# Scores inside blocks of four tokens from one set of products in a hybrid recurrence and attention block

## The chip, the cores and the metric

The kernel runs on one core of one Trainium2 chip. The metric is device microseconds of one execution. A core has TensorE (PE; PEld is its weight load), VectorE (DVE), ScalarE (ACT), GpSimd (POOL) and a queue engine (SP) that issues the transfers. Each engine takes its instructions strictly in order.

## What is computed

A sequence of 1024 tokens (model width 1024) goes through an RMSNorm, one large projection, a gated linear recurrence of 8 heads, a sliding-window attention of 16 heads, a gated merge, an output projection and a last RMSNorm. The change lies in the recurrence. Cut to it, the reference is

```python
f = lb + (1.0 - lb) * jax.nn.sigmoid(hf)      # forget factor, per token and key channel
k_h = 1.0 - f
q_h = jax.nn.silu(hq)
...
b = jnp.cumsum(g_, axis=2)                    # g_ = log f
diff = b[:, :, :, None, :] - b[:, :, None, :, :]
decay = jnp.exp(jnp.where(causal[:, :, None], diff, -jnp.inf))
scores = jnp.einsum('bhtd,bhsd,bhtsd->bhts', q_, k_, decay)
o_intra = jnp.einsum('bhts,bhsv->bhtv', scores, v_)
```

The score of query t and earlier key s is a sum over 128 channels of q times k times the product of all forget factors behind s up to t.

## The kernel before

All products of a weight matrix with the activations are done in float16 with a high and a low part: three passes of eight 128x128 weight tiles (`mm_T`, `mm_tok`; line L302 and L314), 512 or 256 columns each. One unit of 256 weight columns follows the other: for each pair of heads the units `pf` (forget factors), `pq` (queries) and `pv` (values), then gates (`pg`), the attention's keys (`pk`) and values, and so on. ACT and DVE turn each unit's float32 weights into the two float16 parts (`wh` at L235, `wl` at L236) after DVE has found their largest value (`wmx`, L204) and POOL has reduced it over partitions (`p_r`, L121). The product banks are three (`pj`), so a unit's fourth product needs the first one read out.

The recurrence of one head is the generator `hgrn(h)`. It works in the background: `Background.step` lets some of it be issued behind each pass of the foreground. Then the framework's scheduler sets each engine's final order, so every change in the amount of work on an engine can move the others' places.

Inside a head the sequence is eight blocks of 128 tokens (the second half of the token axis lies in reverse order, which is why positions appear in two halves of 512). Scores inside a block are made by distances: `diagonal` multiplies k and q of the same token (L550), and `level` does one set of products for each c of 1, 2, 4, ..., 64 (L582): queries in the second half of each group of 2c tokens with keys in the first half. Between the levels q and k are multiplied in place by products of forget factors (L590 once, then L570 and L573 for each level; the products `hp` come from L540), so that each holds its decay up to the group's border. Before each level ACT copies the half of k and of q that it needs side by side into `kq` (L567, L568, one buffer of three). DVE then keeps what is wanted of each product by a mask, into the score tile `sc` (L554 for the diagonal with mask `idm`, L587 for a level with `lmask[c]`). POOL makes the masks in `setup_masks` at the start. All matrix products of the recurrence are float32 128x128; each is two MATMUL and two LDWEIGHTS records in the trace, and a level is four of them, so eight MATMUL records.

After the seven levels come transposes of k (`tp`, L607), state updates (`up`, L619), a chain of seven state steps on DVE (L627), the readout (`op`, L637 and L639) and its norm (`ms`, `rb`).

Of the kernel before, what the change touches and what calls it, by code (L numbers as in the profile page):

```python
# [14 lines left out]
F32 = mybir.dt.float32  # L15
F16 = mybir.dt.float16
I32 = mybir.dt.int32
U8 = mybir.dt.uint8
AF = mybir.ActivationFunctionType
ALU = mybir.AluOpType  # L20
# [3 lines left out]
P = 128  # L24
# [4 lines left out]
HALF = 512  # L29
# [6 lines left out]
NH = 8  # L36
DH = 64
ZS = 2.0**-19
ARATE = 0.5
ARATE2 = 0.8  # L40
CUT = 4
# [18 lines left out]
def view(ap, off, dims):  # L60

    base = ap[:, off : off + 1]
    return bass.AP(tensor=base.tensor, offset=base.offset, ap=[base.ap[0]] + dims)
# [3 lines left out]
def hybrid_block(ctx: ExitStack, tc: _tile.TileContext, x, norm_w, w_in, hlb, hnw, wbh, sinks, wba, w_out, fnw, out):  # L67
    nc = tc.nc
    V, A, G, PE, SP = nc.vector, nc.scalar, nc.gpsimd, nc.tensor, nc.sync

    const = ctx.enter_context(tc.tile_pool(name="const", bufs=1))
    wp = ctx.enter_context(tc.tile_pool(name="wp", bufs=3))
    sl = ctx.enter_context(tc.tile_pool(name="sl", bufs=24))
    tiny = ctx.enter_context(tc.tile_pool(name="tiny", bufs=4))
# [5 lines left out]
    def nm(s):  # L80
        uid[0] += 1
        return f"{s}{uid[0]}"

    def slot(name, shape=None, dt=F32):
        return sl.tile(shape or [P, 1024], dt, tag="s4", name=nm(name))

    def small(name, w, dt=F32, bufs=4):
        return tiny.tile([P, w], dt, tag=f"{name}_{w}", name=nm(name), bufs=bufs)

    def bank(name, pool=None):  # L90
        pool = pool or sm
        return pool.tile([P, HALF], F32, tag="bk", name=nm(name))
# [42 lines left out]
    ident = const.tile([P, P], F32, name="ident")  # L135
# [226 lines left out]
    lbc = const.tile([P, NH], F32, name="lbc")  # L362
# [1 line left out]
    snk = const.tile([P, 16], F32, name="snk")  # L364
    amask = const.tile([P, 2, 256], F32, name="amask")
    lmask = {}
    idm = const.tile([P, P], U8, name="idm")
    imask = idm[:].rearrange("p (o t) -> p o t", o=1).broadcast_to([P, 4, P])
    sc_bufs = []

    def setup_bounds(dif):

        A.activation(dif[:], dif[:], AF.Sigmoid)
        V.tensor_copy(oml[:], dif[:])
        V.tensor_scalar(lbc[:], dif[:], -1.0, 1.0, ALU.mult, ALU.add)

    def setup_masks():
        for c in (1, 2, 4, 8, 16, 32, 64):
            f = small("mk", P, bufs=1)
            G.memset(f[:], 1.0)  # L380
            J = 64 // c
            fv = f[:].rearrange("p (j e i) -> p j e i", j=J, e=2)
            G.affine_select(fv, fv, [[-2 * c, J], [-c, 2], [0, c]], ALU.is_ge, 0.0, base=0, channel_multiplier=1)
            G.affine_select(fv, fv, [[2 * c, J], [c, 2], [0, c]], ALU.is_ge, 0.0, base=c - 1, channel_multiplier=-1)
            mk = const.tile([P, HALF], U8, name=f"lmask{c}")
            G.tensor_copy(
                mk[:].rearrange("p (m t) -> p m t", m=4),
                f[:].rearrange("p (o t) -> p o t", o=1).broadcast_to([P, 4, P]),
            )
            lmask[c] = mk  # L390
        G.tensor_copy(idm[:], ident[:])
        G.memset(amask[:], 0.0)
        m0, m1 = amask[:, 0], amask[:, 1]

        G.affine_select(m0[:, 0:P], m0[:, 0:P], [[-1, P]], ALU.is_ge, NEG, base=0, channel_multiplier=1)
        G.affine_select(m0[:, P:256], m0[:, P:256], [[-1, P]], ALU.is_ge, NEG, base=P - 2, channel_multiplier=-1)

        G.affine_select(m1[:, 0:P], m1[:, 0:P], [[1, P]], ALU.is_ge, NEG, base=-P, channel_multiplier=1)
        G.affine_select(m1[:, P:256], m1[:, P:256], [[1, P]], ALU.is_ge, NEG, base=0, channel_multiplier=-1)
        for i in range(3):  # L400
            s = slot("sc")
            G.memset(s[:], 0.0)
            sc_bufs.append(s)
# [122 lines left out]
    def hgrn(h):  # L526

        hd = heads[h]  # L530
        q, k, f, v = hd["q"], hd["k"], hd["f"], hd["v"]
        sc = sc_bufs.pop(0)

        hp = tiny.tile([P, 1024], F32, tag="hp", name=nm("hp"), bufs=2)
# [8 lines left out]
            src, at = hp, do  # L543
        prod = hp[:, at : at + NB]

        def diagonal(b):
            lv = bank("lv")
            for j in range(4):
                cs = slice((4 * b + j) * P, (4 * b + j + 1) * P)
                PE.matmul(lv[:, j * P : (j + 1) * P], k[:, cs], q[:, cs], start=True, stop=True)  # L550
            return lv

        def keep_diagonal(b, lv):
            V.copy_predicated(  # L554
                sc[:, b * HALF : (b + 1) * HALF].rearrange("p (c t) -> p c t", c=4), imask,
                lv[:].rearrange("p (c t) -> p c t", c=4),
            )

        def dims_of(c):
            n = 256 // c  # L560
            return [[HALF + c, 2], [2 * c, n], [1, c]], [[HALF - c, 2], [2 * c, n], [1, c]], [[c, 2], [2 * c, n], [1, c]]

        def side_by_side(c):

            kdims, qdims, mdims = dims_of(c)
            kq = tiny.tile([P, 2, HALF], F32, tag="kq", name=nm("kq"), bufs=3)
            A.activation(view(kq[:, 0], 0, mdims), view(k, 0, kdims), AF.Copy)  # L567
            A.activation(view(kq[:, 1], 0, mdims), view(q, c, qdims), AF.Copy)  # L568
            (src, po), n, nb = areas[c.bit_length() - 1], 256 // c, HALF // c
            V.tensor_tensor(  # L570
                view(k, 0, kdims), view(k, 0, kdims), view(src, po + 1, [[nb - 1, 2], [2, n], [0, c]]), ALU.mult
            )
            V.tensor_tensor(  # L573
                view(q, c, qdims), view(q, c, qdims), view(src, po, [[nb + 1, 2], [2, n], [0, c]]), ALU.mult
            )
            return kq

        def level(kq):
            lv = bank("lv")
            for m in range(4):  # L580
                ms = slice(m * P, (m + 1) * P)
                PE.matmul(lv[:, ms], kq[:, 0, ms], kq[:, 1, ms], start=True, stop=True)  # L582
            return lv

        def keep_level(c, lv):
            _, qdims, mdims = dims_of(c)
            V.copy_predicated(view(sc, c, qdims), view(lmask[c], 0, mdims), view(lv, 0, mdims))  # L587

        lv0, lv1 = diagonal(0), diagonal(1)
        V.tensor_tensor(q[:], q[:], f[:], ALU.mult)  # L590
        kq = side_by_side(1)
        yield 1800, 6500
        keep_diagonal(0, lv0)
        keep_diagonal(1, lv1)
        for c in (1, 2, 4, 8, 16, 32, 64):
            lv = level(kq)
            if c < 64:
                kq = side_by_side(2 * c)
            yield 900, LAT
            keep_level(c, lv)  # L600

        kT = slot("kT", [P, NB, P])
        for b in range(2):
            tp = bank("tp")
            w = 4 - b
# [24 lines left out]
        o, osq = kT[:].rearrange("p c d -> p (c d)"), k  # L630
        for b in range(2):
            ps = bank("op")
            for j in range(4):
                p = 4 * b + j
# [19 lines left out]
        for b in range(2):  # L654
            rb = bank("rb")
            for j in range(4):
                p = 4 * b + j
# [16 lines left out]
    def u_ak(blk):  # L674
        c = blk.outscale()
        ainv["k"] = const.tile([P, 1], F32, name="akc")
        V.tensor_scalar(ainv["k"][:], c[:], 0.125 / ZS / ZS, None, ALU.mult)
        for g in range(4):
            kk[g] = slot("kk", [P, 2, T], F16)
        for half in range(2):  # L680
            sli = slice(half * HALF, (half + 1) * HALF)
            for j in range(2):
                ps = bank("pk", pj)
                mm_T(ps[:], blk, j, xact, half * HALF)
                for e in range(2):
                    g = 2 * j + e
                    rows = slice(e * DH, (e + 1) * DH)
                    for d in range(2):
                        A.activation(kk[g][d * DH : (d + 1) * DH, 0, sli], ps[rows], AF.Copy, scale=ZS)
                    for d in range(2):  # L690
                        V.scalar_tensor_tensor(
                            kk[g][d * DH : (d + 1) * DH, 1, sli], ps[rows], ZS, kk[g][rows, 0, sli], ALU.mult,
                            ALU.subtract,
# [4 lines left out]
    def u_av(blk):  # L698
        c = blk.outscale()
        ainv["v"] = const.tile([P, 1], F32, name="avc")  # L700
        V.tensor_scalar(ainv["v"][:], c[:], 1.0 / ZS, None, ALU.mult)
        for e in range(2):
            va[e] = slot("va", [P, NB, 256], F16)
        for tp in range(NB // 2):
            ps = bank("pv", pj)
            psv = ps[:].rearrange("p (t n) -> p t n", t=2)
            for i in range(2):
                mm_tok(psv[:, i], blk, xact, (2 * tp + i) * P)
                bg.step(2780)
            A.activation(va[0][:, 2 * tp : 2 * tp + 2, :], psv, AF.Copy, scale=ZS)  # L710
            V.scalar_tensor_tensor(
                va[1][:, 2 * tp : 2 * tp + 2, :], psv, ZS, va[0][:, 2 * tp : 2 * tp + 2, :], ALU.mult, ALU.subtract
            )
# [210 lines left out]
    sgs, early = {}, {}  # L924
# [162 lines left out]
    with tc.manual_schedule(engines=MANUAL):  # L1087
# [77 lines left out]
        in_turn(tok[4].diag(True), tok[5].diag(True))  # L1165
        in_turn(tok[6].diag(True), tok[7].diag(True))
        setup_bounds(dif)
        n = [0, 0]
        ps1 = [bank("pf", pj), None]
# [21 lines left out]
    late = ExitStack()  # L1191
    for ins in last + (last_all_max[0],):
        late.enter_context(tc.issue_after(ins.ins if hasattr(ins, "ins") else ins))
    setup_masks()
    for half in range(2):
        mmx[half] = const.tile([P, KT], F32, name=f"mmx{half}")

    for i in range(n_last):
# [4 lines left out]
        converts(i + 2)  # L1203
        bg.rate, bg.window = (0.5, 3) if i < n_att else (ARATE if i < n_late else ARATE2, 1)
        if i in (n_heads, n_last_round):
# [27 lines left out]
    for tb in range(NB):  # L1233
        t = slot("xr")
# [3 lines left out]
    for n in range(2):  # L1238
        if n == 1:
            converts(n_out + 4)  # L1240
        for tb in range(NB):
            half = tb // 4
            whole = n == 0 or tb < NB - 1
            for g in ((0, HALF),) if whole else ((0, 256), (256, HALF)):
                ps = bank("po", pj)
                t = 0
                for wi, ai in PASSES:
                    for k in range(KT):
                        w = wout[n][wi][k * 2 // KT][:, k % (KT // 2), g[0] : g[1]]
# [59 lines left out]
```

## Time and profile before

| what | before |
|---|---|
| median of 3 runs | 1214.54 us (1213.32 to 1217.31) |
| the profiled execution's own time | 1214.3 us |
| its span in the trace | 1212.5 us |
| PE, DVE, ACT, POOL busy | 96%, 69%, 45%, 4% of the span |
| granted TensorE clock, mean | 0.992 |

The span is what the trace covers; the execution's own time is 1.8 us more. A busy time is the union of an engine's instructions. [...] In a list of groups each row gives line, engine, operation, output and inputs, shapes, count, busy us and mean ns of one, then the engine's idle time just before them.

### The profile page before, as it was taken

What the parts mean: (1) busy time and instruction counts of PE and PEld (TensorE: products, weight loads), DVE (VectorE), ACT (ScalarE), POOL (GpSimd) and SP (SyncE); (2) the same over time, 40 slices, a digit from 0 to 9 for tenths busy, and PEclk for the clock granted to TensorE, in tenths of its full rate; (3) what the DMA queues carried; (4) which work ended last, traced back from release to release, by engine and by line L of the source; (5) the groups of instructions that cost most, each with busy time, mean ns of one, the idle gap of its engine ahead of it and who ended that gap; (6) DMA issues with size and microseconds to landing.
All of it is one profiled execution on the core that took longest, in us unless ns stands there. A gap on an engine that the chain in (4) does not pass through costs nothing.

```text
span 1212.5 us, 18364 instructions
## 1 busy us (share of the span) xinstructions
PE 1165.0 (96%) x7258; PEld 689.1 (57%) x7258; DVE 832.6 (69%) x1999; ACT 546.9 (45%) x1053; POOL 43.9 (4%) x97
## 2 busy tenths in 40 slices
PE   4999999999999999999999989999897999999997
PEld 3557687687687667675554544445454444444444
DVE  2876955866686778666787774358896877467645
ACT  2733524444353333525864762138677550223323
POOL 0250000000000000000000000000000000000000
PEclk8999999999999999999999999999999999999999
DMA  5121111111111111111453551114455412121312
GB/s 208 36 96 44 35 36 36 35 36 36 35 36 36 35 36 35 36 36 35 108 105 93 113 114 59 55 39 114 106 108 99 111 35 70 35 96 44 139 53 105
DMA packets 132647, 82.48 MB, mean 68 GB/s; under 512 B 81200, under 2 KB 129360, under 8 KB 132560
## 3 DMA queue, kind: packets, MB, share of 16 engines
q1 hardware_dynamic: 132560, 81.30, 24.4%
q8 instruction: 57, 0.93, 0.3%
q14 instruction: 30, 0.25, 0.1%
HBM read 57.17 MB, written 4.19 MB: 51 GB/s over the span
## 4 chain that ended last, share of the span: by engine, by line
PE 77%; DVE 10%; ACT 6%; DMA 5%; issue 2%; SPq 0%; POOL 0%; DVEq 0%; POOLq 0%; ACTq 0%
PE pm L302 19%; PE pg L302 10%; PE pv L314 7%; PE po L1250 7%; PE pq L302 7%; PE paq L302 5%; PE pf L302 5%; PE lv L582 4%; DMA pT<-ph 3%; ACT sp L784 2%; DVE ph L795 2%; PE pk L302 2%; PE pf L1097 1%; DVE sp L774 1%; DMA aot<-ohl 1%
## 5 line engine op out<-in xcount | busy, mean ns | idle before, releaser
L302 PEld LDWEIGHTS <-wh 128*128 128x128 f16 x2304 | 224.3, 98 | 251.4 <-issue 6.2
L302 PEld LDWEIGHTS <-wl 128*128 128x128 f16 x1152 | 112.8, 98 | 129.4
L235 ACT ACTIVATE wh<-raw,p_s 128x512 f16<-128x512 f32 x164 | 104.8, 709 | 119.9 <-issue 42.7
L236 DVE SCALAR_TENSOR_TENSOR wl<-raw,p_s,wh 128x512 f16<-128x512 f32 x164 | 114.2, 749 | 48.5 <-PE pm L302 18.4
L204 DVE TENSOR_REDUCE wmx<-raw 128x1 f32<-128x2048 f32 x45 | 102.7, 2283 | 63.4 <-DMA raw<-in_w_in_dram 42.5
L302 PE MATMUL pm<-hl,wh 128*128 128x512 f16 x512 | 117.0, 379 | 0.0
L1250 PE MATMUL po<-wo,hl 128*128 128x512 f16 (+1 forms) x408 | 83.1, 366 | 0.0
L784 ACT ACTIVATE sp<-sp,anm 128x256 f32<-128x256 f32 (+1 forms) x128 | 61.7, 483 | 25.1 <-DVE anm L779 24.6
L314 PEld LDWEIGHTS <-xh 128*128 128x128 f16 x640 | 62.7, 98 | 7.6
L1250 PEld LDWEIGHTS <-hl 128*128 128x128 f16 x408 | 39.9, 98 | 43.3
L302 PE MATMUL pg<-xh,wh 128*128 128x512 f16 x256 | 60.8, 379 | 0.9 <-DVE qs L731 0.9
L302 PE MATMUL pg<-xl,wh 128*128 128x512 f16 x256 | 61.6, 379 | 0.0
L587 DVE COPY_PREDICATED sc<-lmask,lv 128x512 f32<-128x512 uint8 x56 | 49.5, 886 | 17.6 <-PE lv L582 17.4
L302 PE MATMUL pm<-xh,wh 128*128 128x512 f16 x256 | 61.3, 381 | 0.0
L302 PE MATMUL pm<-xl,wh 128*128 128x512 f16 x256 | 61.3, 379 | 0.0
L302 PE MATMUL pg<-xh,wl 128*128 128x512 f16 x256 | 61.1, 379 | 0.0
L302 PE MATMUL pm<-xh,wl 128*128 128x512 f16 x256 | 60.6, 379 | 0.0
L302 PE MATMUL pm<-hl,wl 128*128 128x512 f16 x256 | 60.5, 379 | 0.0
L582 PEld LDWEIGHTS lv<-kq 128*128 128x128 f32 x448 | 56.6, 192 | 5.0
L582 PE MATMUL lv<-kq 128*128 128x128 f32 x448 | 58.2, 275 | 0.0
L774 DVE CUSTOM_DVE_ANT_0 sp<-as,amask,qsc 128x256 f32<-128x256 f32 (+1 forms) x128 | 52.3, 463 | 4.5 <-DMA pT<-ph 4.2
L567 ACT ACTIVATE kq<-k 128x512 f32<-128x512 f32 x56 | 35.8, 641 | 42.5 <-PE lv L582 37.8
(209 smaller groups left out, 1879.6 us busy)
## 6 DMA issues: line engine op xcount, KB each, us to landing
raw<-in_w_in_dram SPq DMA_DIRECT2D x33, 1024.0 KB, 5.1
xt<-in_x_dram SPq DMA_DIRECT2D x8, 512.0 KB, 6.7
raw<-in_w_branch_hgrn_dram SPq DMA_DIRECT2D x4, 1024.0 KB, 5.2
raw<-in_w_branch_attn_dram SPq DMA_DIRECT2D x4, 1024.0 KB, 5.4
raw<-in_w_out_dram SPq DMA_DIRECT2D x4, 1024.0 KB, 5.1
xr<-in_x_dram SPq DMA_DIRECT2D x8, 512.0 KB, 7.9
out_dram<-xr SPq DMA_DIRECT2D x8, 512.0 KB, 2.6
raw<-in_w_in_dram SPq DMA_DIRECT2D x2, 512.0 KB, 4.1
```

Of the source, the lines that this page charges most:

```text
L204: V.tensor_reduce(mx[:, j : j + 1], self.raw[:, ks], axis=AX.XY, op=ALU.max, apply_absolute_value=True)
L235: A.activation(hi, raw, AF.Copy, scale=s[:])
L236: V.scalar_tensor_tensor(lo, raw, s[:], hi, ALU.mult, ALU.subtract)
L302: PE.matmul(ps, w[:, k, ci * P : (ci + 1) * P], act(ai, k, t0, HALF), start=(n == 0), stop=(n == 3 * KT - 1))
L314: PE.matmul(ps, act(ai, k, t0, P), w[:, k, n0 : n0 + ncol], start=(n == 0), stop=(n == 3 * KT - 1))
L567: A.activation(view(kq[:, 0], 0, mdims), view(k, 0, kdims), AF.Copy)
L582: PE.matmul(lv[:, ms], kq[:, 0, ms], kq[:, 1, ms], start=True, stop=True)
L587: V.copy_predicated(view(sc, c, qdims), view(lmask[c], 0, mdims), view(lv, 0, mdims))
L774: V.tensor_tensor_reduce(self.s[:, i, 0:nk], self.ps[a][:, e * 256 : e * 256 + nk], amask[:, self.n % 2, 0:nk], qsc[:], NEG, ALU.add, ALU. ...
L784: A.activation(self.s[:, i, 0 : self.nk], self.s[:, i, 0 : self.nk], AF.Exp, bias=self.nm[:, i : i + 1], accum_out=self.dn[:, i : i + 1],)
L795: V.scalar_tensor_tensor(self.hl[:, 1], self.s[:, :, 0 : self.nk], 2.0**14, self.hl[:, 0], ALU.mult, ALU.subtract)
L1250: PE.matmul(ps[:, g[0] : g[1]], mact(ai, k, tb * P, P), w, start=(t == 0), stop=(t == 3 * KT - 1))
```

## The change

The diagonal and the levels 1 and 2 become one set of products. Before the diagonal's products are made, `to_middle` takes q and k of each group of four tokens to the middle of the group: at the positions 0, 2 and 3 one of them is multiplied by a forget factor (or by the product of two) and the other by its reciprocal. The products of whole 128-token blocks then hold the right score for any pair of tokens of the same group of four, and the mask `fmask[b]` keeps the lower triangle of each group. `to_ends` multiplies q by the decay from the group's middle on and k by the decay up to its end. The levels go on from 4. The lower bound of f is held above 1e-12.

```diff
+FLOOR = 1e-12
...
-    idm = const.tile([P, P], U8, name="idm")
-    imask = idm[:].rearrange("p (o t) -> p o t", o=1).broadcast_to([P, 4, P])
+    fmask = []
...
+        V.tensor_scalar(lbc[:], lbc[:], FLOOR, None, ALU.max)
 
     def setup_masks():
-        for c in (1, 2, 4, 8, 16, 32, 64):
+        for b in range(2):
+            f = small("mk", P, bufs=1)
+            G.memset(f[:], 1.0)
+            fv = f[:].rearrange("p (j i) -> p j i", i=4)
+            G.affine_select(fv, fv, [[-4, 32], [-b, 4]], ALU.is_ge, 0.0, base=0, channel_multiplier=1)
+            G.affine_select(fv, fv, [[4, 32], [1 - b, 4]], ALU.is_ge, 0.0, base=3 * b, channel_multiplier=-1)
+            mk = const.tile([P, P], U8, name=f"fmask{b}")
+            G.tensor_copy(mk[:], f[:])
+            fmask.append(mk)
+        for c in (4, 8, 16, 32, 64):
...
+        def at_token(t, p):
+            return view(t, p, [[HALF + 3 - 2 * p, 2], [4, P]])
+
+        early = view(hp, 0, [[257, 2], [2, P], [0, 4]])
+        late = view(hp, 1, [[255, 2], [2, P], [0, 4]])
+
+        def to_middle():
+            inv = tiny.tile([P, 3, 2, P], F32, tag="kq", name=nm("inv"), bufs=3)
+            f1, f2, f23 = at_token(f, 1), at_token(f, 2), view(hp, 1, [[255, 2], [2, P]])
+            for i, (p, w, up, down) in enumerate(((0, f1, k, q), (2, f2, q, k), (3, f23, q, k))):
+                V.reciprocal(inv[:, i], w)
+                V.tensor_tensor(at_token(up, p), at_token(up, p), w, ALU.mult)
+                V.tensor_tensor(at_token(down, p), at_token(down, p), inv[:, i], ALU.mult)
+
+        def to_ends():
+            dims = [[HALF, 2], [4, P], [1, 4]]
+            V.tensor_tensor(view(q, 0, dims), view(q, 0, dims), early, ALU.mult)
+            V.tensor_tensor(view(k, 0, dims), view(k, 0, dims), late, ALU.mult)
...
+        to_middle()
         lv0, lv1 = diagonal(0), diagonal(1)
-        V.tensor_tensor(q[:], q[:], f[:], ALU.mult)
-        kq = side_by_side(1)
+        to_ends()
+        kq = side_by_side(4)
         yield 1800, 6500
         keep_diagonal(0, lv0)
         keep_diagonal(1, lv1)
-        for c in (1, 2, 4, 8, 16, 32, 64):
+        for c in (4, 8, 16, 32, 64):
```

Line numbers of the changed kernel are higher: L550 becomes L581, L582 L613, L590 L574 and L575, L570 and L573 become L601 and L604, L554 L585, L587 L618; the reciprocals are L568, the products of `to_middle` L569 and L570.

The scheduler's order changes with it. On **PE**, in the unit `pf` of the second pair of heads, the diagonal of head 1 (q_648, k_194) stood 16 foreground products behind that of head 0, between two of the unit's passes:

```order
L302 MATMUL pf_1019<-xh,wl_775 128x512
L550 MATMUL lv_1076<-q_648,k_194 128x128 x4
L550 MATMUL lv_1081<-q_648,k_194 128x128 x4
L302 LDWEIGHTS wh_774
L302 MATMUL pf_1098<-xh,wh_774 128x512
```

Now the diagonal of head 0 stands where it stood, and that of head 1 (now q_647, k_193) 85 foreground products behind it, inside a pass with `wl` weights:

```order
L303 MATMUL pf_1234<-xh,wl_774 128x512
L581 MATMUL lv_1096<-q_647,k_193 128x128 x4
L581 MATMUL lv_1101<-q_647,k_193 128x128 x4
L613 MATMUL lv_1138<-kq_1057 128x128 x4
L303 LDWEIGHTS wl_774
L303 MATMUL pf_1234<-xh,wl_774 128x512
```

It moved back by 69 products of 512 columns. In the other three pairs the distance is 85, 90 and 92.

On **DVE**, behind the first diagonal (head 0 is q_647, k_192 before), stood:

```order
L554 COPY_PREDICATED sc_612<-idm,lv_1036 128x512
L590 TENSOR_TENSOR q_647<-q_647,f_191 128x1024
L570 TENSOR_TENSOR k_192<-k_192,f_191 128x2x256
L554 COPY_PREDICATED sc_612<-idm,lv_1041 128x512
L573 TENSOR_TENSOR q_647<-q_647,f_191 128x2x256
L570 TENSOR_TENSOR k_192<-k_192,hp_1028 128x2x128x2
L204 TENSOR_REDUCE wmx_1504<-raw_1264 128x1
L573 TENSOR_TENSOR q_647<-q_647,hp_1028 128x2x128x2
```

and now (head 0 is q_646, k_191, head 1 q_647, k_193):

```order
L585 COPY_PREDICATED sc_611<-fmask_560,lv_1045 128x512
L574 TENSOR_TENSOR q_646<-q_646,hp_1027 128x1024
L575 TENSOR_TENSOR k_191<-k_191,hp_1027 128x1024
L585 COPY_PREDICATED sc_611<-fmask_566,lv_1050 128x512
L604 TENSOR_TENSOR q_646<-q_646,hp_1027 128x2x64x4
L568 RECIPROCAL inv_1086<-f_192 128x256 x2
L568 RECIPROCAL inv_1086<-hp_1078 128x256
L601 TENSOR_TENSOR k_191<-k_191,hp_1027 128x2x64x4
L205 TENSOR_REDUCE wmx_1517<-raw_1285 128x1
L477 TENSOR_SCALAR f_1014<-sg_1113,oml,lbc 128x512
L570 TENSOR_TENSOR q_647<-q_647,inv_1086 128x2x128
L570 TENSOR_TENSOR k_193<-k_193,inv_1086 128x2x128
```

So the second head's three reciprocals stand between the two diagonals, behind the first head's work; three more products of `to_middle`, a second TENSOR_SCALAR of `f` and two scalars follow before the second diagonal's inputs are whole.

On **POOL**, among the masks, the maximum of the weights of the first `pv` unit (p_r_626) stood behind the third mask's first selection:

```order
L386 CAST lmask_566<-mk_562 128x512
L380 MEMSET mk_568 128x128
L383 AFFINE_SELECT mk_568<-mk_568 128x128
L121 ISA p_r_626<-wmx_624 128x1
L384 AFFINE_SELECT mk_568<-mk_568 128x128
L386 CAST lmask_572<-mk_568 128x512
L121 ISA p_r_765<-wmx_763 128x1
```

and now (p_r_625) it stands behind the sixth mask's selections:

```order
L396 CAST lmask_584<-mk_580 128x512
L390 MEMSET mk_586 128x128
L393 AFFINE_SELECT mk_586<-mk_586 128x128
L394 AFFINE_SELECT mk_586<-mk_586 128x128
L122 ISA p_r_625<-wmx_623 128x1
L396 CAST lmask_590<-mk_586 128x512
L122 ISA p_r_764<-wmx_762 128x1
```

It moved behind thirteen more instructions of mask making, three masks and a part.

## Rows read from the trace of the kernel before

**Rows 1.** The page: head, busy times, and the chain that ended last.

```profile
span 1212.5 us, 18364 instructions
...
PE 1165.0 (96%) x7258; PEld 689.1 (57%) x7258; DVE 832.6 (69%) x1999; ACT 546.9 (45%) x1053; POOL 43.9 (4%) x97
...
PE pm L302 19%; PE pg L302 10%; PE pv L314 7%; PE po L1250 7%; PE pq L302 7%; PE paq L302 5%; PE pf L302 5%; PE lv L582 4%; DMA pT<-ph 3%; ACT sp L784 2%; DVE ph L795 2%; PE pk L302 2%; PE pf L1097 1%; DVE sp L774 1%; DMA aot<-ohl 1%
```

**Rows 2.** Busy time by stretches; first row: what the columns are.

```profile
core 0: us, PE busy (x) PEld busy (x) DVE busy (x) ACT busy (x) POOL busy (x), PEclk, DMA share, GB/s
...
61.00:506.00 445.00, 445.00 (x3027) 318.32 (x3026) 323.48 (x659) 186.15 (x322) 21.50 (x43) 1.00 0.12 39
102.00:150.00 48.00, 48.00 (x294) 31.13 (x293) 44.74 (x70) 27.46 (x47) 1.07 (x2) 1.00 0.14 45
150.00:200.00 50.00, 50.00 (x397) 40.92 (x396) 23.86 (x67) 16.64 (x32) 0.45 (x1) 1.00 0.12 39
...
506.00:553.00 47.00, 46.04 (x328) 32.52 (x328) 33.89 (x62) 19.91 (x28) 1.02 (x3) 1.00 0.14 46
553.00:977.00 424.00, 405.00 (x2608) 204.95 (x2608) 296.65 (x867) 237.45 (x522) 6.01 (x15) 0.99 0.40 90
```

**Rows 3.** Chain of waits around 100 to 134 us: start, length, what.

```profile
115.03 0.89 PE lv L582 x8
...
120.02 1.78 PE lv L582 x16
```

**Rows 4.** Groups of instructions of PE: the levels' products.

```profile
L582 PE MATMUL lv<-kq 128*128 128x128 f32 x448 | 58.2, 275 | 0.0
```

**Rows 5.** Groups of instructions of DVE.

```profile
L590 DVE TENSOR_TENSOR q<-q,f 128x1024 f32<-128x1024 f32 x8 | 9.8, 1221 | 0.5 <-PE lv L550 0.5
...
L570 DVE TENSOR_TENSOR k<-k,hp 128x512 f32<-128x512 f32 x48 | 33.2, 692 | 0.7 <-ACT kq L567 0.6
...
L830 DVE TENSOR_TENSOR ohl<-ao,ohl 128x256 f16<-128x256 f32 x32 | 13.4, 420 | 4.6 <-ACT ohl L827 3.9
...
L131 DVE RECIPROCAL p_s<-p_inv 128x1 f32<-128x1 f32 x52 | 8.3, 160 | 0.9
...
L802 DVE RECIPROCAL adn<-adn 128x4 f32<-128x4 f32 x32 | 5.5, 172 | 0.2
...
L554 DVE COPY_PREDICATED sc<-idm,lv 128x512 f32<-128x512 uint8 x16 | 11.7, 729 | 1.0 <-PE lv L550 0.9
...
L204 DVE TENSOR_REDUCE wmx<-raw 128x1 f32<-128x2048 f32 x45 | 102.7, 2283 | 63.4 <-DMA raw<-in_w_in_dram 42.5 <-DMA raw<-in_w_branch_attn_dram 8.6 <-DMA raw<-in_w_out_dram 8.1
...
L468 DVE TENSOR_SCALAR f<-sg,oml,lbc 128x512 f32<-128x512 f32 x16 | 9.9, 618 | 4.4 <-ACT sg L466 4.3
```

**Rows 6.** DVE in order of time: head 0's levels 1 and 2 kept.

```profile
117.63 1.31 DVE L587 COPY_PREDICATED sc<-lmask,lv 128x512 f32<-128x512 uint8 x1
...
122.70 1.29 DVE L587 COPY_PREDICATED sc<-lmask,lv 128x512 f32<-128x512 uint8 x1
```

**Rows 7.** Groups of instructions of ACT.

```profile
L567 ACT ACTIVATE kq<-k 128x512 f32<-128x512 f32 x56 | 35.8, 641 | 42.5 <-PE lv L582 37.8 <-DVE k L570 3.5 <-DVE p_u L129 0.7
...
L608 ACT ACTIVATE kT<-tp 128x512 f32<-128x512 f32 x8 | 4.8, 597 | 17.6 <-PE tp L607 17.6
```

**Rows 8.** POOL in order of time among the masks.

```profile
67.10 0.36 POOL L121 PARTITION_ALL_REDUCE p_r<-wmx  x1 [0.84 <-DVE wc L246]
67.34 0.70 POOL L384 TENSOR_SCALAR_AFFINE_SELECT mk<-mk 128x128 f32<-128x128 f32 x1
...
75.31 0.63 POOL L384 TENSOR_SCALAR_AFFINE_SELECT mk<-mk 128x128 f32<-128x128 f32 x1
```

**Rows 9.** ACT in order of time: weights of the first values unit.

```profile
72.55 2.56 ACT L235 ACTIVATE wh<-raw,p_s 128x512 f16<-128x512 f32 x4 [4.70 <-DVE p_s L131]
```

**Rows 10.** The chain over the whole span: first queries and values units.

```profile
61.58 20.29 PE pq L302 x94
81.87 20.96 PE pv L314 x192
```

More of the change, by code (lines that the diff above doesn't have):

```diff
@@ L390, in setup_masks @@
             lmask[c] = mk
-        G.tensor_copy(idm[:], ident[:])
         G.memset(amask[:], 0.0)
@@ L554, in keep_diagonal @@
             V.copy_predicated(
-                sc[:, b * HALF : (b + 1) * HALF].rearrange("p (c t) -> p c t", c=4), imask,
+                sc[:, b * HALF : (b + 1) * HALF].rearrange("p (c t) -> p c t", c=4), view(fmask[b], 0, [[0, 4], [1, P]]),
                 lv[:].rearrange("p (c t) -> p c t", c=4),
```

## The prediction

> **What bounds the kernel now.** I read the page first: PE is busy for 96% of the span, DVE for 69%, ACT for 45%, and the levels' products alone are 4% of the chain that ended last [rows 1]. Such an average mixes stages, so the second view is the busy time by stretches. The recurrence of all eight heads lies between 61 and 506 us. There PE is busy for 445.0 of 445 us, DVE for 323.5, ACT for 186, at a granted clock of 1.00 [rows 2]. A PE that is always busy could still be waiting inside long records, since the ends of products are modelled; the third view answers that. In the chain of waits a level, eight MATMUL records of float32, takes 0.89 us where it stands alone, and two levels in a row take 1.78 us [rows 3]: the same 111 ns per record, with the next product right behind. So in this stretch the products follow each other at PE's own pace and nothing else sets the time. What leaves PE there leaves the run, unless something new makes PE wait.
>
> **What the change takes from PE.** There are 448 such records: 8 heads, 7 levels, 8 records [rows 4]. The change removes levels 1 and 2 of every head and leaves the diagonal's products as they are, only masked otherwise. That is 16 levels at 0.89 us [rows 3]: 14.2 us. (The mean of 275 ns in the group's row is no price: records overlap, and 128 of them at 275 ns would be 35 us.)
>
> **What it takes from and adds to DVE.** Per head it removes the multiplication of all q (1.22 us, the 1024-wide row), four multiplications 512 wide (0.69 us each, 2.77) [rows 5], and the keeping of levels 1 and 2, where runs of one or two elements cost more than the later ones: 1.31 and 1.29 us [rows 6]. Together 6.6 us. It adds six multiplications 256 wide, for which I take the 0.42 us of another 256-wide tensor-tensor row (2.5 us), and two 1024 wide at 1.22 us (2.4 us) [rows 5]: 5.0 us. And three reciprocals, 256 wide. The trace has reciprocals of one element (160 ns) and of four (172 ns) alone [rows 5]. Lower bound: the rate of a multiplication, 0.42 us. Upper bound from these rows: 12 ns for three more elements are 4 ns an element, so 160 + 255 x 4 = 1180 ns. I take 0.44, the multiplication plus some fixed excess, because the nearest shape in width is the 256-wide multiplication, and keep 1.18 for the range. So the net per head is between 6.2 - 6.6 = -0.4 us and 8.5 - 6.6 = +1.9 us; for eight heads -3 to +15 us.
>
> DVE has the room: 445 - 323 = 122 us idle in the stretch, 107 behind the cut. The tightest part is 102 to 150 us, where two heads run at once: 44.7 of 48 us, but the next 50 us hold only 23.9 [rows 2]. With the upper bound the two heads add 3.8 us there, less than the 26 us that follow. That is the cover; were it gone, each us that DVE is late with weights or with reading out the three product banks would be one of PE.
>
> [...]
>
> **ACT and the masks.** ACT loses four copies per head, 0.64 us each [rows 7]: off the path, worth nothing. The new tile of reciprocals takes one of the three `kq` buffers in turn, but two levels less need one, so the ring is shorter than before. The masks on POOL are as many as before, two of them smaller. But the order puts the maximum of the first values unit's weights behind thirteen more mask instructions. In the trace that maximum ran at 67.10 us; the moved ones ran from 67.34 to 75.94, with other work and an idle time between them [rows 8], and the two smaller masks give some back: I take 6 us later. Its weights were then made from 72.55 to 75.11 [rows 9], and would now be ready at 81.1. The unit starts at 81.87 [rows 10]. Nothing, with 0.8 us to spare. Reading out the first of the query products also stands behind that maximum on DVE: it would come at about 74, and the fourth product of that unit needs the bank at 61.58 + 3/4 of 20.29 = 76.8 [rows 10]. If POOL is 3 us later than that, PE loses about 2 us once. I keep 2 us for the range.
>
> **Two places where PE could wait in order.** The second head's diagonal now stands 85 products behind the first one's. At 216 ns (pq's 94 records in 20.29 us [rows 10]) that is 18.4 us. In that time DVE must do: two keepings at 0.73, two products at 1.22, two at 0.69, the weight maximum at 2.28, two `f` at 0.62, five 256-wide products at 0.42 and two scalars at 0.15 us, 11.1 us [rows 5], and three reciprocals: 12.4 us with 0.44, 14.6 with the upper bound. It is covered by 4 to 6 us. Later, transposes and state updates of both heads of the first pair stand together without foreground products; an update needs ACT's copy of its transposes, 0.60 us [rows 7], and three other groups of transposes run meanwhile. Nothing again.
>
> **Sum.** PE -14.2 us, POOL's order 0 (up to +2), DVE 0, ACT 0. The profiled execution took 1214.3 us, which is 0.24 below the median of the runs; 1214.3 - 14.2 = 1200.1, and at the median 1214.5 - 14.2 = 1200.3 us. What lies behind 506 us, the attention and the merges, has the same order as before and should only start earlier. PE stands still there for 1.0 us until 553 and for 19 us until 977 [rows 2], waiting for transfers and short chains, and these may fall a little otherwise: I allow 2 us either way.
>
> **The rivals.**
>
> *The reciprocals are long,* near 2.4 us. Then 11.1 + 3 x 2.4 = 18.3 us: the second diagonal just makes it. But in the first pair three of them stand ahead of two weight maxima, 3 x 2.0 = 5.9 us, and with POOL's 6 us the first values weights could be up to 12 us later instead of 6: 87 against 81.9, 5 us lost. Time 1200 to 1205, in the middle 1202.8. For it: nothing in the trace has this width; against it: 4 ns an element at most. [...] Chance 0.12.
>
> *Slower: PE stands at the second diagonals.* The same place, with reciprocals beyond 2.4 us each, or DVE late by as much for another reason. Each of the four pairs then pays 3 x (r - 2.4) us, since the foreground products behind the diagonal wait too. It decides from 12 x (r - 2.4) = 14.2 + 3.6, r = 3.9 us or 15 ns an element; at r = 5 it is 31 us, 1231 us. Against it: four times the upper bound of the rows. Chance 0.04.
>
> *No gain: the time is given back.* The stages behind 506 us could be held by something that doesn't start earlier, a transfer or a chain, so that only the heads' stretch is shorter; 1211 to 1217 us. For it: these stages have 20 us of waits. Against it: PE is busy for 405 of 424 us there, and the 16 DMA engines for 0.12 of the time in the heads' stretch [rows 2], so loads are not what paces it. Chance 0.05.
>
> *The later stages fall otherwise,* and 3 to 8 us are lost or won there: 1194 to 1197 or 1204 to 1209. Chance 0.05.
>
> **Numbers.** The forecast, 1200.3 us, has 0.74. Its own range is 1197 to 1204: the 2 us of later stages and 1 us of stalls won, 2 us of POOL and 2 us of later stages lost. With the long reciprocals it reaches 1205.5; no more than 0.15 is left out. The kernel's measurement can tell about 0.3%, 3.6 us, from no change. Faster by more: 0.74 + 0.12 + 0.05 = 0.91; within it 0.05; slower 0.04.
>
> **What would show it.** In the changed profile: 320 records of level products instead of 448; PE still busy for all of the heads' stretch, which ends near 492 instead of 506; no rise of PE's idle time before the second diagonals; the reciprocals' row near 0.4 us (up to 1.2); DVE's sum within -3 to +15 us; the first values unit starting at about 82. Wrong would be: reciprocals over 2.4 us, PE waiting for DVE in the heads' stretch, or the gap of 14 us shrinking between 506 and the end.

## The result and the profile after

| what | before | after |
|---|---|---|
| median of 5 runs | 1214.54 us | 1200.46 us (1199.07 to 1202.10) |
| ratio to before, 95% interval | 1 | 0.9879 (0.9862 to 0.9896) |
| span of the profiled execution | 1212.5 us | 1198.8 us |
| PE, DVE, ACT busy | 1165.0, 832.6, 546.9 us | 1150.4, 860.6, 527.1 us |

The change takes 14.1 us off the median; 14.2 were forecast. (Of all executions below, one took 2504 us, among ten of the kernel with the addition alone; no ratio counts it.) The page's head and busy times, which answer to [rows 1]:

```profile
span 1198.8 us, 18078 instructions
...
PE 1150.4 (96%) x7130; PEld 671.7 (56%) x7130; DVE 860.6 (72%) x2032; ACT 527.1 (44%) x1021; POOL 46.3 (4%) x96
```

PE has 128 records less and is busy for 14.6 us less; DVE is busy for 28 us more. The busy times by stretches, with the same columns as [rows 2]; the heads' stretch now ends at 492 us:

```profile
61.00:492.00 431.00, 431.00 (x2910) 303.18 (x2908) 349.60 (x698) 163.19 (x285) 24.25 (x39) 1.00 0.12 40
102.00:150.00 48.00, 48.00 (x278) 28.88 (x276) 43.79 (x67) 23.61 (x40) 1.89 (x2) 1.00 0.14 45
150.00:200.00 50.00, 50.00 (x414) 42.68 (x413) 35.44 (x92) 16.39 (x31) 0.36 (x1) 1.00 0.10 32
...
492.00:540.00 48.00, 46.75 (x320) 31.47 (x319) 36.85 (x57) 23.82 (x34) 1.03 (x3) 1.00 0.14 45
540.00:963.00 423.00, 404.30 (x2605) 204.40 (x2604) 295.51 (x866) 236.65 (x521) 6.01 (x15) 0.99 0.40 90
```

PE is busy for 431.0 of 431 us there, as it was for 445 of 445, while DVE rose from 323.5 to 349.6 us, from 73% of the stretch to 81%. Its tightest 48 us are no fuller than before; the 50 us behind them rose from 23.9 to 35.4. Behind 540 us the busy times are those of before within 1.2 us, and PE's idle time there is 18.7 us (19.0 before).

The groups of instructions that answer to [rows 4, 5], products first:

```profile
L613 PE MATMUL lv<-kq 128*128 128x128 f32 x320 | 40.3, 275 | 0.0
...
L618 DVE COPY_PREDICATED sc<-lmask,lv 128x512 f32<-128x512 uint8 x40 | 28.3, 715 | 0.2 <-PE lv L613 0.2
...
L568 DVE RECIPROCAL inv<-f 128x256 f32<-128x256 f32 x16 | 27.0, 1721 | 0.0
...
L568 DVE RECIPROCAL inv<-hp 128x256 f32<-128x256 f32 x8 | 13.8, 1719 | 0.0
...
L570 DVE TENSOR_TENSOR k<-k,inv 128x256 f32<-128x256 f32 x16 | 10.3, 645 | 0.0
L574 DVE TENSOR_TENSOR q<-q,hp 128x1024 f32<-128x1024 f32 x8 | 9.8, 1219 | 0.6 <-PE lv L581 0.5
...
L575 DVE TENSOR_TENSOR k<-k,hp 128x1024 f32<-128x1024 f32 x8 | 9.7, 1216 | 0.0
```

The reader sees the two sizes that the forecast had wrong: a reciprocal of 256 elements takes 1.72 us, and a 256-wide product of `to_middle` 0.65, not 0.42.

The chain of waits from 60 to 180 us, in order of time (start, length, what), shows where the two heads' diagonals stand:

```profile
...
61.69 20.29 PE pq L303 x94
81.98 20.96 PE pv L315 x192
102.94 1.73 PE pf L303 x8
104.66 1.78 PE lv L581 x16
106.45 18.35 PE pf L303 x85
124.79 1.78 PE lv L581 x16
126.58 0.89 PE lv L613 x8
...
```

Each piece begins where the last ended: nothing but PE's own products is on the chain, and a level is 0.89 us as in [rows 3]. The same view has the first product of the attention's queries, before and after, which marks the end of the heads' stretch below:

```profile
553.30 20.88 PE paq L302 x96
```

```profile
539.50 20.88 PE paq L303 x96
```

DVE in order of time between the two diagonals; the first keeping, the reciprocals and the last input of the second diagonal:

```profile
105.70 0.73 DVE L585 COPY_PREDICATED sc<-fmask,lv 128x512 f32<-128x512 uint8 x1
...
109.98 3.36 DVE L568 RECIPROCAL inv<-f 128x256 f32<-128x256 f32 x2
113.25 1.69 DVE L568 RECIPROCAL inv<-hp 128x256 f32<-128x256 f32 x1
...
120.78 0.62 DVE L569 TENSOR_TENSOR q<-q,hp 128x256 f32<-128x256 f32 x1
```

That input is ready at 121.40; the diagonal comes at 124.79, so 3.4 us were left. On POOL the maximum of the first values unit's weights came at 70.55 us instead of 67.10 [rows 8]. ACT made those weights from 78.17 on, in one piece with the next unit's:

```profile
70.55 0.36 POOL L122 PARTITION_ALL_REDUCE p_r<-wmx  x1 [0.80 <-DVE wc L247]
```

```profile
78.17 5.01 ACT L236 ACTIVATE wh<-raw,p_s 128x512 f16<-128x512 f32 x8 [0.59 <-DVE p_s L132]
```

What POOL reduces there is DVE's maximum over each partition (`wmx`). It stands in the trace before, and in the trace after behind the first head's three reciprocals, as

```profile
64.73 2.27 DVE L204 TENSOR_REDUCE wmx<-raw 128x1 f32<-128x2048 f32 x1
```

```profile
68.18 2.27 DVE L205 TENSOR_REDUCE wmx<-raw 128x1 f32<-128x2048 f32 x1
...
74.57 1.42 DVE L512 SCALAR_TENSOR_TENSOR q<-pq,wc,sg 128x512 f32<-128x512 f32 x2
```

It ended at 67.00 before and at 70.45 now, and POOL's instruction followed 0.1 us later both times, after POOL had stood idle for 0.84 and 0.80 us. So DVE set that time, and not the masks. The last line is the reading out of the first query products.

### The profile page after: what moved, and what is told of

It reads as the page before. It is cut to its first block, busy times and chain, and to the rows that moved or that the text cites. A ratio compares the mean times of both kernels' runs of the same rounds, so it can differ in the third digit from the quotient of the medians.

```text
span 1198.8 us, 18078 instructions
## 1 busy us (share of the span) xinstructions
PE 1150.4 (96%) x7130; PEld 671.7 (56%) x7130; DVE 860.6 (72%) x2032; ACT 527.1 (44%) x1021; POOL 46.3 (4%) x96
## 4 chain that ended last, share of the span: by engine, by line
PE 76%; DVE 10%; ACT 6%; DMA 5%; issue 2%; SPq 0%; POOL 0%; DVEq 0%; POOLq 0%; ACTq 0%
PE pm L303 19%; PE pg L303 11%; PE pv L315 7%; PE po L1282 7%; PE pq L303 7%; PE pf L303 5%; PE paq L303 5%; PE lv L613 3%; DMA pT<-ph 3%; ACT sp L816 2%; PE pk L303 2%; DVE ph L827 2%; DMA aot<-ohl 2%; PE pf L1129 1%; DVE sp L806 1%
## 5 line engine op out<-in xcount | busy, mean ns | idle before, releaser
L237 DVE SCALAR_TENSOR_TENSOR wl<-raw,p_s,wh 128x512 f16<-128x512 f32 x164 | 114.1, 748 | 45.1 <-PE pm L303 18.6
L122 POOL PARTITION_ALL_REDUCE p_r<-wmx x47 | 26.6, 570 | 872.6 <-DVE wmx L205 656.3
L497 ACT ACTIVATE sg<-pg,wc 128x512 f32<-128x512 f32 x32 | 21.9, 683 | 47.0 <-PE pg L303 46.9
L315 PE MATMUL pv<-wh,xl 128*128 128x256 f16 x320 | 42.0, 273 | 0.0
L315 PE MATMUL pv<-wh,xh 128*128 128x256 f16 x320 | 41.6, 273 | 0.0
```

The source lines that it names most:

```text
L122: last_all_max[0] = G.partition_all_reduce(r[:], mx, channels=P, reduce_op=bass_isa.ReduceOp.max)
L237: V.scalar_tensor_tensor(lo, raw, s[:], hi, ALU.mult, ALU.subtract)
L315: PE.matmul(ps, act(ai, k, t0, P), w[:, k, n0 : n0 + ncol], start=(n == 0), stop=(n == 3 * KT - 1))
L497: A.activation(sg[:], ps[:], AF.Sigmoid, scale=c[:])
```

## Experiments

All ran beside the kernel before; ratios are to it.

**The removed products put back.** Only PE's work is restored, in `diagonal`, whose products are made twice into the same banks:

```diff
-            for j in range(4):
+            for j in (0, 1, 2, 3) * 2:
```

> The changed kernel with the products of each head's diagonal issued twice into the same banks: 64 more float32 products, as many as levels 1 and 2 had; DVE, ACT and POOL do the same. Theory PE (in the heads' stretch only PE's own pace sets the time): 16 x 0.89 us come back, 1200.5 + 14.2 = 1214.7 us, as before the change. Rival DVE/ACT (the gain came from the keepings and copies that were dropped): 1200 to 1204 us.

Measured: 1215.5 us, ratio 1.0005 (0.9996 to 1.0014). The time came back whole, with the change's lighter ACT and heavier DVE left as they are. The chain of waits there shows each diagonal twice as long and everything behind it later by that:

```profile
...
105.66 3.57 PE lv L581 x32
109.23 18.34 PE pf L303 x85
127.58 3.57 PE lv L581 x32
...
```

So the gain is the removed products' own time on PE. The keepings and copies that went with them are worth nothing here.

**Only the removal.** The kernel before, without the copies, products and keepings of levels 1 and 2; the scores of these distances are left out:

```diff
-        kq = side_by_side(1)
+        side_by_side(1)
+        side_by_side(2)
+        kq = side_by_side(4)
...
-        for c in (1, 2, 4, 8, 16, 32, 64):
+        for c in (4, 8, 16, 32, 64):
             lv = level(kq)
```

with the two copies in `side_by_side` made for c above 2 alone.

> The kernel before with levels 1 and 2 left out and nothing put in their place: no copies, no products, no keeping; q and k are still multiplied as before. (The scores of neighbours at these distances are missing.) Theory PE: 1214.5 - 14.2 = 1200.3 us, the same as the change, since the 1.72 us reciprocals and the 0.63 us products that the change adds are covered. Rival (the added DVE work costs something on the path, and the change gained more than it shows): below the change by that, 1195 to 1198 us.

Measured: 1200.2 us, ratio 0.9881 (0.9866 to 0.9896), the change's own figure. What the change adds costs nothing that these runs can measure. DVE is busy for 303 us of the heads' 431 here, 46 us less than in the change:

```profile
61.00:492.00 431.00, 431.00 (x2911) 305.43 (x2910) 303.40 (x650) 161.54 (x285) 24.67 (x43) 1.00 0.12 40
```

**Only the addition.** The kernel before with the reciprocals and six products written to a tile that nobody reads:

```diff
...
+        for p, w in ((0, at_token(f, 1)), (2, at_token(f, 2)), (3, view(hp, 1, [[255, 2], [2, P]]))):
+            V.reciprocal(inv[:, 0], w)
+            V.tensor_tensor(dead, at_token(k, p), w, ALU.mult)
+            V.tensor_tensor(dead, at_token(q, p), inv[:, 0], ALU.mult)
         lv0, lv1 = diagonal(0), diagonal(1)
```

> The kernel before, with the reciprocals and the six 256-wide products of the change added ahead of each diagonal into a tile that nobody reads: about 3 x 1.72 + 6 x 0.63 = 8.9 us of DVE per head, 71 us in all, two and a half times what the change adds in sum. Theory PE: 1214.5 us within 2 us, DVE at about 89% of the heads' stretch. Rival (DVE work in this stretch is partly on the path): at a tenth of it 1221 us, at a third 1238 us.

Measured: 1213.9 us, ratio 0.9996 (0.9986 to 1.0007). Some 58 us more of DVE (323.5 to 381.6) in the heads' stretch, where 71 were expected from the records' lengths, and no change in the time. PE waits nowhere in the stretch:

```profile
61.00:506.00 445.00, 445.00 (x3030) 317.80 (x3028) 381.59 (x732) 187.09 (x323) 21.42 (x43) 1.00 0.12 38
```

**A copy in place of each reciprocal.** The scores inside groups of four are then not the reference's.

```diff
-                V.reciprocal(inv[:, i], w)
+                V.tensor_copy(inv[:, i], w)
```

> The changed kernel with a copy in place of each reciprocal (so the scores inside groups of four are not the reference's): some 30 us less of DVE. Theory (DVE is covered): 1200.5 us, no change. Rival (the long reciprocals cost part of the gain): 1196 to 1199 us.

Measured: 1202.2 us, ratio 0.9904 (0.9880 to 0.9927), whose interval overlaps the change's. A copy takes 0.29 to 0.40 us, and DVE was busy for 27 us less than in the change (833.5 against 860.6); that won nothing.

**Each reciprocal twice, and three times.**

```diff
                 V.reciprocal(inv[:, i], w)
+                V.reciprocal(inv[:, i], w)
```

> The changed kernel with each reciprocal done twice: 24 x 1.72 = 41 us more of DVE, 390 of 431 us in the heads' stretch, 90%. The order moves the second head's diagonal further back (110 to 146 products instead of 85 to 92) and the first pair's first diagonal forward, to the start of the first values unit. Theory (DVE is covered while it has room): the heads' stretch stays PE's, but for a few us at that early diagonal: 1200 to 1208 us. Rival (the second diagonals wait, 3 x (3.4 - 2.1) us in each of four pairs): 1216 us.

> The changed kernel with each reciprocal done three times: 83 us more of DVE than the change, 432 us of work in a stretch of 431. Theory (PE's pace holds only while DVE has room): DVE sets the time now, PE waits at the diagonals, 15 to 30 us are lost, 1215 to 1230 us. Rival (DVE is not on the path of this stretch at all): 1200 to 1204 us.

Measured: twice 1204.8 us, ratio 0.9917 (0.9900 to 0.9933); three times 1227.3 us, ratio 1.0102 (1.0085 to 1.0119). The first lost some 4 us against the change, and its waits of PE in the heads' stretch, 3.2 us, name the place (engine, line, what it waited for: us in total, times, longest):

```profile
PE pq L303 <- DVE q L512: 2.8, 1, 2.8
PE lv L582 <- DVE hp L550: 0.4, 1, 0.4
```

The long one is for the reading out of the first query products, which stands on DVE behind the first head's reciprocals; the 0.4 us are at the first diagonal of the first pair, where the expectation had put the loss. The second diagonals don't wait. With three, the same view shows PE waiting at five places:

```profile
PE lv L583 <- DVE hp L550: 5.8, 1, 5.8
PE tp L641 <- DVE k L603: 5.7, 1, 5.7
PE op L673 <- DVE f L661: 3.5, 1, 3.5
PE pq L303 <- DVE q L512: 3.2, 1, 3.2
PE pk L303 <- DVE kk L725: 0.4, 1, 0.4
```

The diagonal that waits here (L583) is again the first one of the first pair; the others are transposes (`tp`), readouts (`op`), the first query products and a unit of the attention's keys. That is 18.6 us of waits, and the stretch is no longer PE's:

```profile
61.00:519.00 458.00, 439.41 (x2901) 306.22 (x2900) 422.49 (x734) 167.31 (x292) 19.13 (x39) 0.98 0.12 38
```

The mean granted clock of the stretch was 0.98 of full speed, where the change had 1.00: around three of these waits the granted clock was 0.5, for 6.8, 3.4 and 6.8 us. The diagonal that had waited shows it, with 3.75 us instead of 1.78:

```profile
93.29 3.75 PE lv L583 x16
```

With the 18.6 us of waits and some part of what half the clock over these 17.1 us can cost (8.5 us at the most, an estimate: half of 17.1) one comes near the 26.9 us that this kernel loses against the change. So DVE can hold PE back in this stretch, as the slower rival says; it was busy for 92% of it then. Between 89 and 92% nothing was measured. The scheduler had made room for them: in the chain of waits the second head's diagonal begins 20.1, 26.5 and 26.0 us behind the first head's in the last three pairs of the change, 25.5, 34.7 and 37.7 us with each reciprocal twice, 35.2, 42.9 and 44.6 us with three; in the first pair the first diagonal moved too, forward from 104.66 us to 86.66 and 93.29. The places that waited are therefore others than the rival named.

**Widths and steps.** Operations whose results nobody reads, in the last head, four of each; `one`, `two` and `four` are steps over 256 elements, and `n` is 256:

```diff
...
+                V.tensor_tensor(d[:, 0:n], f[:, 0:n], hp[:, 0:n], ALU.mult)
+                V.tensor_tensor(view(d, 0, two), view(f, 0, two), view(hp, 0, two), ALU.mult)
+                V.tensor_tensor(d[:, 0:n], view(f, 0, four), hp[:, 0:n], ALU.mult)
...
+                V.tensor_tensor(view(d, 0, four), f[:, 0:n], hp[:, 0:n], ALU.mult)
...
+                V.reciprocal(d[:, 0:64], f[:, 0:64])
+                V.reciprocal(d[:, 0:n], f[:, 0:n])
+                V.reciprocal(d[:, 0:512], f[:, 0:512])
```

> The changed kernel with 36 dead operations in the last head: 256-wide products with steps of 1, 2 and 4 elements on the read and the written side, and reciprocals 64, 256 and 512 wide, all contiguous. If the 0.63 us of the change's products comes from the step of four elements, those of step 1 and 2 take 0.42 us and those of step 4 0.6 us or more; if it comes from two runs per instruction or from neighbours on the memory, all take the same. Reciprocals by 6.1 ns an element: 0.54, 1.72 and 3.3 us. The time as a whole is of no interest, some us more.

It ran once (1207.0 us), for these durations alone. The groups of DVE (L626 steps of 1, L627 steps of 2 on all three sides, L628 a step of 4 on one read side, L630 on the written side alone):

```profile
L634 DVE RECIPROCAL dead<-f 128x512 f32<-128x512 f32 x4 | 13.4, 3353 | 0.0
...
L633 DVE RECIPROCAL dead<-f 128x256 f32<-128x256 f32 x4 | 7.0, 1750 | 0.0
...
L630 DVE TENSOR_TENSOR dead<-f,hp 128x256 f32<-128x256 f32 x4 | 2.5, 619 | 0.0
L628 DVE TENSOR_TENSOR dead<-f,hp 128x256 f32<-128x256 f32 x4 | 2.5, 618 | 0.0
...
L632 DVE RECIPROCAL dead<-f 128x64 f32<-128x64 f32 x4 | 2.2, 548 | 0.0
L626 DVE TENSOR_TENSOR dead<-f,hp 128x256 f32<-128x256 f32 x4 | 1.7, 426 | 0.0
L627 DVE TENSOR_TENSOR dead<-f,hp 128x256 f32<-128x256 f32 x4 | 1.7, 426 | 0.0
```

A step of four float32 elements on a read side or on the written side cost 0.19 us at this width (0.62 against 0.43); a step of two cost nothing (0.43 both). Reciprocals took 6.3 ns an element between 64 and 512 ((3353 - 548) / 448).

**Blocks of eight.** The same idea one level further: level 4 goes too, and the products are brought to the middle of eight tokens.

```diff
...
-            for i, (p, w, up, down) in enumerate(((0, f1, k, q), (2, f2, q, k), (3, f23, q, k))):
+            for i, (p, w) in enumerate((
+                (2, at_token(f, 3)), (1, pair(1)), (0, (at_token(f, 1), pair(1))),
+                (4, at_token(f, 4)), (5, pair(2)), (6, (at_token(f, 6), pair(2))), (7, view(hp, 513, [[127, 2], [2, 64]])),
+            )):
...
-        for c in (4, 8, 16, 32, 64):
+        for c in (8, 16, 32, 64):
```

> The same idea for blocks of eight tokens: level 4 goes too; seven positions of eight are taken to the middle, 128 wide each. Theory PE: 8 x 0.89 = 7.1 us less than the change, 1193.3 us, up to 1196 where DVE (some 3 us more per head) makes PE wait once or twice. Rival (DVE now sets the time in the heads' stretch): 1200 us or more.

Measured: 1198.1 us, ratio 0.9862 (0.9848 to 0.9877): 2.3 us below the change, with intervals that overlap, and 2 us less gain than the low end of what the theory gave. From the first query product to the first attention query product on the chain of waits (`pq` to `paq`) it took 470 us, the change 478: the 7 to 8 us are there. From there to the output projection it took 573 us, the change 569. So a part is given back behind the heads. To see whether that belongs to the kernel, both ran again on one chip.

> The changed kernel once more, on the same chip as the next run, to set the two side by side: 1200.5 us. Its profile shows what of the stages behind the heads differs from one execution to the next: if the idle time and the low-clock spans there are the same as in its first profile (18 us, two spans of 3.4 us), they belong to the kernel.

> The kernel with blocks of eight once more. Theory (its products save 7 to 8 us in the heads' stretch, and the order of its later stages gives some 4 us back): 1198 us, 2 to 3 below the change, with 20 us of idle time and more than two low-clock spans behind the heads again. Rival (the loss in the later stages was chance in the one profiled execution and the gain is smaller for another reason): idle time of 18 us there and still 1198 us, or a median near 1193 us.

Measured: the change 1202.8 us, ratio 0.9898 (0.9880 to 0.9916); blocks of eight 1196.7 us, ratio 0.9850 (0.9834 to 0.9867). The intervals are apart: blocks of eight is the faster version, by about 6 us here and 2 in the medians of the earlier runs. Neither side of the expectation came as it was put: the median lies between 1198 and 1193 us, the idle time below between 20 and 18 us. Its later part took 572.6 us, the change 570.6 this time. The busy times from the first attention query product on, over stretches of 428 us (blocks of eight, second profile) and 425 us (the change, second profile):

```profile
532.00:960.00 428.00, 409.15 (x2610) 206.36 (x2610) 296.62 (x867) 238.24 (x524) 6.97 (x15) 0.98 0.40 89
```

```profile
541.00:966.00 425.00, 406.83 (x2608) 205.12 (x2606) 295.89 (x865) 236.47 (x520) 6.99 (x15) 0.99 0.40 90
```

PE's idle time is 18.9 and 18.2 us, less than a microsecond apart, and for the same work (2610 and 2608 records) PE is busy for 2.3 us more at a lower mean clock (0.98 against 0.99). In the clock's records there were 17.1 us at a granted clock of 0.5 in that part for blocks of eight (13.7 in its first profile), and 10.2 us for the change (6.8 in its first). By this account, an estimate, most of what blocks of eight give back is time at the low clock, which also differs from one execution to the next: three stretches of 3.4 us for the change here, two in its first profile. No run tests it, and why there is more of it with blocks of eight is open.

## Why the prediction was right

**What bounds the kernel.** Right, and shown: products put back on PE cost what they had saved (ratio 1.0005), while 58 us more of DVE cost nothing (0.9996), and 27 us less than in the change gained nothing.

**PE's term.** 16 levels at 0.89 us, 14.2 us: measured 14.1 in the medians, 13.7 in the spans. From `pq` to `paq`, 61.58 to 553.30 us before and 61.69 to 539.50 after, the chain shortened from 491.7 us to 477.8. The price taken from the chain of waits was the right one; the group's mean of 275 ns still stands at 275.

**DVE's terms were mis-sized.** The step "the nearest shape in width is the 256-wide multiplication" took 0.44 us for a reciprocal and 1.18 as an upper bound; it is 1.72. The rows of one and of four elements, 12 ns apart, gave 4 ns an element; over 64 to 512 elements it is 6.3, so the upper bound was none. The other row, 0.42 us for a 256-wide product, was of contiguous elements, and the change steps over four: 0.61 to 0.65. DVE's forecast of -3 to +15 us became +28 in busy time; the sum of the lengths with the measured prices is +38, and busy time, which counts overlapping records once, is less. It did not matter, because the room in which it had to fit, 107 us, was read from the right place.

**POOL's order.** The time is nearly right and the reason is wrong. Six microseconds later were taken for POOL's maximum behind thirteen more mask instructions, and 3.5 came; but POOL stood idle for 0.8 us just before it and waited for DVE's maximum, which came 3.45 us later behind the first head's reciprocals. With copies in their place DVE's maximum ended at 67.69 us and POOL, busy with masks, took it up at 68.78: in that run the masks did cost time, 1.1 us. Another 2.2 us came between POOL's maximum and the weights, where products of `to_middle` and a second readout now stand on DVE ahead of the scale. So the weights began at 78.17 us, near the 78.6 of the forecast's working by luck. The unit started at 81.98 us (81.87 before): nothing, as forecast, with no wait of PE. The readout of the first query products came at 74.57 us, where the forecast had about 74, and its bank was needed at 76.8: this is the place where the run with each reciprocal twice loses.

**The second diagonals.** The cover was 18.35 us (18.4 forecast), the work 15.7 us instead of 12.4 to 14.6 (the terms of the forecast's 11.1 us add up to 11.2), the margin 3.4 us instead of 4 to 6; 0.7 us of that margin comes from DVE beginning before the cover did.

**The rivals.** The long reciprocals came nearer in size than the forecast's 0.44 (1.72 measured, 2.4 supposed, which no row or run shows), and not in time: nothing waited for the first values weights. With each reciprocal done twice PE does lose time near there, 2.8 us, but at the first query products' readout, which the forecast had priced under POOL's order. The slower rival's break-even was given as 3.9 us a reciprocal. In effect 3.4 us (twice) cost 4.4 us against the change, and 5.2 us (three times) 26.9 us, which is 13.1 us more than the kernel before (1214.2 us beside it). So the break-even lies between the two, as the rival had it. Its own sum, 12 reciprocals by what each is over 2.4 us, gives 12.5 and 33 us: too much both times, and for a place that did not wait, since the scheduler had moved the diagonals. That time is given back behind the heads did not happen for the change: from `paq` to the output projection it took 569 us before and after.

## What to carry to other kernels

Price a removed piece by its length in the chain of waits, in the stretch where it stands, and check that the stretch is that engine's alone; then work added to another engine can be free, whatever its sum over the whole run says: here 58 us fitted into 122 us of idle time. It is not free up to the last idle microsecond, for at 89% busy one early readout came late. A rate can't be read from two instructions of a few elements each (4 ns an element here, 6.3 measured), and a row of contiguous elements does not price one that steps over four (0.43 against 0.62 us). Where such a price is unknown, read the room it has to fit in, and test the limit by doubling the work. And where an engine stands idle just before a moved instruction, as POOL did here for 0.80 us, the move is not what sets its time: look at what it waits for.

## What was not expected

A float32 product on DVE whose operand steps over four elements, on a read or on the written side alone, took 0.62 us at 256 elements, against 0.43 with steps of one or two. A reciprocal took 0.55, 1.75 and 3.35 us at 64, 256 and 512 elements. And at a load of DVE of 89% of the stretch (reciprocals twice) the loss was 4 us, and 2.8 of the 3.2 us of PE's waits were at one early readout; with three times the reciprocals PE waited at five places of the stretch, 18.6 us in all, and the mean granted clock was 0.98 instead of 1.00.
